# Sample attention's value products: one visit of eight quads per batch instead of four of two, and the mixed rows loaded and split at other pairs

## The chip, the cores and the metric

The kernel runs on one NeuronCore of a Trainium2 chip. A core has five engines that run side by side, each in its own program order: TensorE (PE in the profile, its weight loads PEld), VectorE (DVE), ScalarE (ACT), GpSimd (POOL) and SyncE (SP), which here issues nearly all DMAs. The metric is the device time of one execution in microseconds, the median of several runs.

## The reference, cut to what matters

One step of a decoder layer for two groups: a prompt of 1024 tokens and 8 sample batches of 4 tokens. The change is in the attention of the samples. Each sample attends to its 4096 past tokens (32 pages of 128) and its new ones; keys and values come from a cached latent of 256 numbers and a rope key of 32 per token:

```python
def one(args):                       # one sample batch
    pages, q1, c1, pe1 = args
    c_all = concatenate([pool_ckv[pages].reshape(4096, 256), c1])
    pe_all = concatenate([pool_kpe[pages].reshape(4096, 32), pe1])
    k, v = mla_keys_values(c_all, pe_all, k_pos, w_uk, w_uv, g_qk_k)
    return masked_attend(q1, k, v, q_pos, k_pos)   # 8 heads, 4 queries, softmax(q k) v
```

`k` is RMS-normalised per head (hence sums of squares of `c @ w_uk`), and `v = c @ w_uv`. The kernel never builds `v`: it multiplies the probabilities with the latents themselves and applies `w_uv` to the result.

## The kernel before, in words

The stage is `phase2b`. Its unit is a **quad**, four pages of one batch; a batch has eight quads and there are 64 in all. A **pair** is two pages, so a quad has two pairs, a batch 16 and the stage 128. The function `steps` walks over the pairs `n`, and writes down the work of each engine in the order in which it will run: PE, ACT, DVE and POOL follow that order by hand (`manual_schedule`), while SP's DMAs are placed by a planner.

For each pair `pair_score` issues 24 score matmuls on PE (line 186, tile `s`, 12 of 288 columns and 12 of 256), two squares on ACT (L1452, L1455), an addition on DVE (L1454) and, one pair later, a reduction of the squares on DVE (L1458). Every second pair starts with a rope matmul (L1422). For each quad ACT casts the latents (L1403), POOL and DVE subtract the rounded part (L1407), POOL rotates the rope key (L1392 to L1394), and ACT and DVE sum its square (L1415, L1416).

A batch's softmax (`batch_softmax`, steps r = 0 to 13) is spread over its pairs 12 to 21; pairs from 16 on belong to the next batch's scores. Steps 0 to 8 are mostly DVE work on the norms and the maximum (L1469, L247 to L261, L1476, L1479), with a scaling on POOL. Then PE transposes the maximum (r = 9, L1508, pair 19), DVE reduces it and writes it as a diagonal `dg` (r = 10, L1511 and L1513), PE spreads that over all partitions (r = 11, L1516, behind pair 20's scores), ACT copies it, POOL subtracts it (L1528) and ACT takes the exponential (L1524, pair 21).

The value products follow `LAG` = 4 pairs behind: with `v = n - 16 - LAG`, `quad_pv` multiplies a quad's probabilities with its cached rows `ck`, four matmuls of a 32-column arrangement, one per page (L1537; the profile has two records of each). The first quad of a batch has one more for the new tokens (L1535). All of a batch adds up in one PSUM bank, tile `o`. A **visit** is a stretch of such matmuls between score matmuls: now after every fourth pair, two quads each, so four visits a batch, behind its pairs 23, 27, 31 and 35 (counted from the batch's first), which are pairs 7, 11, 15 and 3 of the batch whose scores run then. After the last one `batch_out` copies `o` (ACT, L1545), sums the denominators (PE, L1549, DVE L1551 and L1555), and `batch_close` folds the result (PE L1561, ACT L1562).

The cached rows live in 15 buffers of the tag `ck`; a quad's buffer comes free when its visit is done. A column of ones in it (POOL's memset, L1284) is set shortly before the visit. The same tag also serves for other data: `mixed_load` brings in rows of another part of the layer (L1225, 384 KB, four times, one each in the score pairs of batches 1 to 4), which `split` then turns into a rounded part (ACT, L205) and a rest (DVE, L208), two halves per load. `quad_load` issues a quad's 8 page DMAs on SP (L1375 for `cT`, L1379 for `ck`), three quads ahead.

Behind pair 127 the planner also orders PE, ACT, DVE and POOL, and the work of `mem_kv` (L1605 and on) is mixed with the last batch's softmax.

Of the kernel before, what the change touches and what calls it, by code (L numbers as in the profile page):

```python
# [15 lines left out]
NB, ND = 8, 4  # L16
# [138 lines left out]
class Net:  # L155
# [1024 lines left out]
    def phase2b(self):  # L1180
        nc, tc, I = self.nc, self.tc, self.I
# [4 lines left out]
        ppt, pp = self.open("ps3t", space=PSUM), self.open("ps3", space=PSUM)  # L1186
# [10 lines left out]
        cosT, sinT, quads = self.cosT, self.sinT, self.quads  # L1197

        LAG, AHEAD = 4, 3
        last = NB * 16  # L1200
        st, ev, late = {}, {}, []

        def at(n, pos, f, *a):
            ev.setdefault((n, pos), []).append(lambda: f(*a))

        def run(n, pos):
            for f in ev.pop((n, pos), []):
                f()
# [13 lines left out]
        def mixed_load(k):  # L1222

            raw = place()[:, :768].rearrange("p (k n) -> p k n", k=2)
            nc.sync.dma_start(raw, self.mix_dram[:, k : k + 2, :384])  # L1225
            for e in range(2):
                at(8 * k + 24 + 2 * e, 3, lambda e: self.split(*(x[:, k + e] for x in self.mx0), raw[:, e], self.col("g_ab", k + e)), e)

        for k in range(0, 8, 2):
            at(8 * k + 20, 0, mixed_load, k)  # L1230
        at(last - 4, 3, lambda: self.split(*wk0, raws[0].rearrange("p (k n) -> p k n", k=8)))
        for b in range(NB):
            n = b * 16
            at(n - 10, 0, lambda b: st.__setitem__(b, self.batch_open(p, b)), b)
            at(n - 8, 2, lambda b: self.batch_enter(st[b], b), b)
            for r, (k, pos) in enumerate(((12, 0), (13, 0), (14, 0), (14, 3) if b == NB - 1 else (15, 0), (15, 0) if b == NB - 1 else (15, 3), (16, 0), (17, 0), (17, 3), (18, 2), (19, 2), (20, 0), (20, 2), (21, 3))):
                f = lambda b=b, r=r: self.batch_softmax(p, ppt, st[b], r, b == NB - 1)
                if n + k <= last:
                    at(n + k, pos, f)
                else:  # L1240
                    late.append(f)
            if b < NB - 1:
                at(n + 21, 0, lambda b=b: self.batch_softmax(p, ppt, st[b], 13, False))
            n += 16 + LAG + 15
            tail = (
                lambda b=b: self.batch_out(pt, st[b], 0),
                lambda b=b: self.batch_out(pt, st[b], 1, ppt, b == NB - 1),
                lambda b=b: self.batch_close(pt, ppt, b, st.pop(b)),
            )
            for k, pos, f in ((0, 3, tail[0]), (2, 2, tail[1]), (3 if b == NB - 2 else 4, 3, tail[2])):  # L1250
                if b < NB - 1:
                    at(n + k, pos, f)
# [4 lines left out]
        def steps(n0, n1):  # L1257
            for n in range(n0, n1):
                Q, v = n // 2, n - 16 - LAG
                if n >= 16 and n % 2 == 0 and Q + AHEAD < NB * 8:  # L1260
                    quads[Q + AHEAD] = self.quad_load(p, Q + AHEAD)
                for k, dst, src in ((2, b4, self.b_dram), (16, self.fold4, I["c_fold4"]), (64, wuv, I["w_uv"])):
                    if n == k:
                        self.behind(nc.sync.dma_start(dst, src), self.page_dma[-1])
                if n > last - 8 and n % 2 == 0 and len(raws) < 4:
                    raw = place()[:, : 8 * P]
                    src = (I["w_mk"][0], I["memT"][:, :4], I["memT"][:, 4:], I["w_mk"][1])[len(raws)]
                    nc.sync.dma_start(raw.rearrange("p (k n) -> p k n", n=src.shape[2]), src)
                    raws.append(raw)
                for pos in (-2, -1, 0):  # L1270
                    run(n, pos)
                if n % 2 == 0 and 0 <= Q + 1 < NB * 8:
                    at(n + 1, -2, self.quad_prep(quads[Q + 1]))
                    at((6, 8, 10, 10, 11)[Q + 1] if Q < 4 else n + 3, 0, self.quad_sums, Q + 1, quads[Q + 1], st[(Q + 1) // 8])
                if n % 2 and 0 <= Q + 2 < NB * 8:
                    self.quad_rot(Q + 2, quads[Q + 2], cosT, sinT)
                if n in (-1, 1, 3, 5, 7, 9, 11, 13):
                    k = Q + 4
                    rvs[k] = rvs.get(k) or self.quad_pages(k)
                    quads[k] = self.quad_load(None, k, None, rvs[k])  # L1280
                for k in {1: (0,), 3: (1,), 4: (2,), 5: (3,), 6: (4,), 7: (5,), 9: (6,), 11: (7,), 12: (8,), 13: (9,), 14: (10,)}.get(n, ()):
                    self.quad_load(p, k, quads[k], rvs.get(k))
                if n % 2 and 0 <= v + 1 < last:
                    nc.gpsimd.memset(quads[(v + 1) // 2]["ck"][:, :, 256:257], 1.0)  # L1284
                run(n, 1)
                if 0 <= n < last:
                    rope = (Q + 1, quads[Q + 1], st[(Q + 1) // 8]) if n % 2 and Q + 1 < NB * 8 else None
                    for f in self.pair_score(p, pp, n, quads[n // 2], st[n // 16], rope):
                        at(n + 1, -1, f)
                elif n == -1:  # L1290
                    self.quad_rope(self.t(pp, [P, 2, 512], F32, "s", 2)[:, 0, 320:448], 0, quads[0], st[0])()
                run(n, 2)
                if 0 <= v < last and v % 4 == 3:
                    for z in (v // 2 - 1, v // 2):
                        self.quad_pv(ppt, z, quads.pop(z), st[v // 16])
                run(n, 3)

        with tc.manual_schedule(engines={E.PE, E.Activation, E.DVE, E.Pool}):
            steps(-10, last + 1)

        with tc.manual_schedule(engines={E.SP}):
            self.close("ps3")
            for x in ("p3a", "p3c", "sq", "sm"):
                self.close(x)
            self.wr = self.open("wr", bufs=3, side="right")
            self.wp = self.open("w", bufs=3, side="right")
            mem = self.mem_kv(raws, wk0)
            for f in late[:3]:
                f()
            next(mem)  # L1310
            steps(last + 1, last + 4)
            for _ in range(5):
                next(mem)
            steps(last + 4, last + 7)
            for f in late[3:]:
                f()
            for _ in range(6):
                next(mem)
            steps(last + 7, last + 16 + LAG)
            for _ in mem:  # L1320
                pass
# [1191 lines left out]
```

## Time and profile before

| | |
|---|---|
| median of 3 runs | 1827.79 us (1826.15 to 1829.96) |
| profiled execution, span | 1823.1 us |
| sample attention, scores of batches 0 to 7 | 402 to 848 us of the span |
| matmuls of the visits (L1537) | 512 records, 380 ns each (median) |
| one mixed load to landing | 4.7 us (median of 4) |

The span is from the first to the last instruction of one execution; the median has what lies around it as well. In rows of time order the first number is the start in microseconds from the span's start, the second the duration; `xN` merges N instructions of one line; in brackets stands the engine's idle time ahead of it and what ended it. The starts of successive matmuls, and not their durations, tell what PE's time goes to, since they overlap: a score matmul lasts 0.28 to 0.30 us in the profile, but the next starts 0.12 to 0.13 later.

### The profile page before, as it was taken

The numbers are of one execution on the slowest core, as the hardware profiler recorded it, in microseconds if no ns is written. First come the engines' busy times: TensorE is split into PE (matmuls) and PEld (weight loads), VectorE is DVE, ScalarE is ACT, GpSimd is POOL, SyncE is SP. The second block draws the span as 40 slices with busy tenths as digits, with TensorE's granted clock in tenths as the row PEclk, the third lists the DMA queues.
The fourth block names the chain that finished last, engine by engine and source line by source line (L and its number), as shares of the span: only waits on it lengthen the run. The fifth ranks groups of instructions, "written<-read, shape, count | busy, mean of one in ns | idle before, by whom it ended". The sixth has DMA issues, their size and how long they took to land.

```text
span 1823.1 us, 39307 instructions
## 1 busy us (share of the span) xinstructions
PE 1800.6 (99%) x14226; PEld 1700.3 (93%) x14226; DVE 1349.6 (74%) x2796; ACT 921.5 (51%) x1910; POOL 703.0 (39%) x861
## 2 busy tenths in 40 slices
PE   9999999999999999999999999999999999999999
PEld 8999777779999999998899979999999999999999
DVE  7864767657778776777645767998888888888664
ACT  7435676766655555556433556533333333344442
POOL 1021655534545444544023010377667776400000
PEclk9999999999999999999999999999999999999999
DMA  8102354558866766664645156222222222595242
GB/s 323 47 18 70 117 176 127 165 181 227 220 201 189 202 189 181 178 180 127 194 152 188 36 197 196 71 71 94 83 71 71 83 71 85 152 325 162 85 149 78
DMA packets 153187, 261.18 MB, mean 143 GB/s; under 512 B 20897, under 2 KB 97538, under 8 KB 152994
## 3 DMA queue, kind: packets, MB, share of 16 engines
q1 hardware_dynamic: 152130, 257.63, 45.4%
q8 instruction: 112, 1.84, 0.4%
q10 hardware_dynamic: 864, 1.05, 0.2%
q14 instruction: 81, 0.66, 0.1%
HBM read 212.79 MB, written 45.82 MB: 142 GB/s over the span
## 4 chain that ended last, share of the span: by engine, by line
PE 81%; DVE 3%; ACT 1%; issue 1%; SPq 1%; POOL 1%; DMA 0%; DVEq 0%; ACTq 0%; POOLq 0%
PE s L186 22%; PE d L186 12%; PE b L186 8%; PE F L186 7%; PE X L186 7%; PE E L186 7%; PE A L186 3%; PE y L186 3%; PE o L1047 2%; PE o L1537 2%; PE tp L1032 1%; PE tp L186 1%; PE s L1422 1%; PE tp L985 1%; PE t L186 1%
## 5 line engine op out<-in xcount | busy, mean ns | idle before, releaser
L186 PE MATMUL s<-w2h,ch 128*128 128x256 f32 x1018 | 301.9, 297 | 0.5 <-ACT S L1425 0.5
L186 PE MATMUL s<-w2h,cl 128*128 128x256 f32 x1018 | 293.2, 288 | 0.0
L186 PE MATMUL s<-w2l,ch 128*128 128x256 f32 x1018 | 292.9, 288 | 0.0
L186 PEld LDWEIGHTS s<-w2h,ch 128*128 128x128 f32 x1018 | 191.5, 188 | 8.9 <-issue 3.7
L186 PEld LDWEIGHTS s<-w2l,ch 128*128 128x128 f32 x1018 | 191.7, 188 | 0.0
L186 PEld LDWEIGHTS s<-w2h,cl 128*128 128x128 f32 x1018 | 191.3, 188 | 0.0
L1458 DVE TENSOR_REDUCE ss<-sq 128x16 f32<-128x1024 f32 x128 | 155.3, 1213 | 29.8 <-ACT sq L1455 29.4
L1407 POOL TENSOR_TENSOR cl<-cT,ch 128x512 fp32r<-128x512 f32 x64 | 83.5, 1304 | 185.6 <-ACT ch L1403 185.4
L1455 ACT ACTIVATE sq<-s 128x512 f32<-128x512 f32 x128 | 76.6, 598 | 82.7 <-PE s L186 82.7
L1452 ACT ACTIVATE sq<-s 128x512 f32<-128x512 f32 x128 | 76.9, 601 | 75.9 <-PE s L186 70.9
L201 ACT CAST a<-brb 128x528 fp32r<-128x528 f32 x77 | 48.8, 634 | 110.5 <-PE d L186 104.6
L186 PE MATMUL d<-a,w 128*128 128x264 f32 x768 | 95.2, 284 | 0.0
L202 DVE TENSOR_TENSOR a<-brb,a 128x528 fp32r<-128x528 f32 x77 | 54.1, 704 | 55.2 <-ACT a L201 55.1
L186 PEld LDWEIGHTS d<-a,w 128*128 128x128 f32 x768 | 94.3, 188 | 0.0
L2149 POOL TENSOR_TENSOR lo<-s,hi 128x1024 fp32r<-128x1024 f32 x20 | 64.0, 3200 | 45.7 <-ACT hi L2148 45.7
L186 PE MATMUL mm<-whi,xh 128*128 128x256 f32 (+3 forms) x272 | 77.1, 285 | 0.0
L2204 ACT COPY a<-A 128x264 f32<-128x264 f32 x43 | 16.1, 375 | 120.6 <-PE A L186 114.2
L186 PE MATMUL mm<-wlo,xh 128*128 128x256 f32 (+3 forms) x272 | 76.8, 285 | 0.1
L186 PE MATMUL mm<-whi,xl 128*128 128x256 f32 (+3 forms) x272 | 76.8, 286 | 0.0
L1403 ACT CAST ch<-cT 128x512 fp32r<-128x512 f32 x128 | 73.5, 629 | 0.0
L2270 POOL TENSOR_TENSOR cv<-cv,row 128x1056 f32<-128x1056 f32 x22 | 65.1, 2960 | 21.0 <-ACT cv L2269 21.0
L186 PE MATMUL d<-a,hi 128*128 128x264 f32 x552 | 72.0, 284 | 0.0
(755 smaller groups left out, 6348.1 us busy)
## 6 DMA issues: line engine op xcount, KB each, us to landing
cT<-cT SPq DMA_DIRECT2D x256, 160.0 KB, 2.8
ck<-ck SPq DMA_DIRECT2D x256, 144.0 KB, 3.4
raw<-w_up SPq DMA_DIRECT2D x44, 512.0 KB, 3.5
wsumd<-wsum SPq DMA_DIRECT2D x26, 512.0 KB, 3.9
actd<-cv SPq DMA_DIRECT2D x44, 264.0 KB, 2.4
brb<-actd SPq DMA_DIRECT2D x44, 264.0 KB, 5.7
wsum<-w_down SPq DMA_DIRECT2D x22, 512.0 KB, 3.8
raw<-wsumd SPq DMA_DIRECT2D x20, 512.0 KB, 3.7
```

The source lines that it names most:

```text
L186: x = self.nc.tensor.matmul(out, l, r, start=first and i == 0, stop=last and i == len(seq) - 1)
L201: first = {"act": nc.scalar.copy, "pool": nc.gpsimd.tensor_copy, "dve": nc.vector.tensor_copy}[eng](hi, src)
L202: low = lambda: nc.vector.tensor_tensor(lo, src, hi, ALU.subtract)
L1047: nc.tensor.matmul(u["o"][g : g + 64, o : o + m * P], s["v"][:, j, h % 4], th[:, z * P : (z + m) * P], start=j == 0, stop=b == len(banks) - 1,
L1403: nc.scalar.copy(d["h"][:, k], src[k])
L1407: (nc.vector if k else nc.gpsimd).tensor_tensor(d["l"][:, k], src[k], d["h"][:, k], ALU.subtract)
L1452: nc.scalar.activation(sq[:, 0], ps[:, :, n0 : n0 + 256], AF.Square)
L1455: nc.scalar.activation(sq[:, 1], pt.rearrange("p (e d) -> p e d", e=2), AF.Square)
L1458: yield lambda: nc.vector.tensor_reduce(s["ss"][:, g0 : g0 + 2].rearrange("p e (z h) -> p z e h", z=2), sq.rearrange("p z e (h d) -> p z e ...
L1537: nc.tensor.matmul(s["o"][j * 32 : j * 32 + 32], S[:, q * 4 + j], d["ck"][:, j, :257], start=q == 0 and j > 0, stop=q == 7)
L2149: eng.tensor_tensor(lo, src, hi, ALU.subtract)
L2270: nc.gpsimd.tensor_tensor(cv, cv, row, ALU.mult)
```

## The change

All eight quads of a batch are multiplied in one visit, where the first of the four visits stood (`v % 16 == 3`, pair 23 from the batch's first, which is pair 7 of the next one). Batch 6 (`NB - 2`) does six quads there and holds two for `v % 16 == 15`. `batch_out` and `batch_close` come 12 pairs earlier, except for batch 6. The memset of the ones comes 12 pairs earlier per quad. The mixed rows are loaded at pair `8k + 24` instead of `8k + 20`, and their halves are split at pairs `8k + 26` and `8k + 27` instead of `8k + 24` and `8k + 26`.

```diff
             for e in range(2):
-                at(8 * k + 24 + 2 * e, 3, lambda e: self.split(*(x[:, k + e] for x in self.mx0), raw[:, e], self.col("g_ab", k + e)), e)
+                at(8 * k + 26 + e, 3, lambda e: self.split(*(x[:, k + e] for x in self.mx0), raw[:, e], self.col("g_ab", k + e)), e)
 
         for k in range(0, 8, 2):
-            at(8 * k + 20, 0, mixed_load, k)
+            at(8 * k + 24, 0, mixed_load, k)
...
-            n += 16 + LAG + 15
+            n += 16 + LAG + (15 if b == NB - 2 else 3)
...
-                if n % 2 and 0 <= v + 1 < last:
-                    nc.gpsimd.memset(quads[(v + 1) // 2]["ck"][:, :, 256:257], 1.0)
+                if n % 2 and 0 <= n - 7 < last:
+                    nc.gpsimd.memset(quads[(n - 7) // 2]["ck"][:, :, 256:257], 1.0)
...
-                if 0 <= v < last and v % 4 == 3:
-                    for z in (v // 2 - 1, v // 2):
-                        self.quad_pv(ppt, z, quads.pop(z), st[v // 16])
+                if 0 <= v < last and v % 16 in (3, 15):
+                    b, held = v // 16, 2 if v // 16 == NB - 2 else 0
+                    for z in range(b * 8, b * 8 + 8 - held) if v % 16 == 3 else range(b * 8 + 8 - held, b * 8 + 8):
+                        self.quad_pv(ppt, z, quads.pop(z), st[b])
```

## The prediction, made before the change was run

> **What bounds the kernel now.** I read the page's head first, then the busy time by stretches, the order of time on PE, and the order of time on DVE.
>
> ```profile
> span 1823.1 us, 39307 instructions
> PE 1800.6 (99%) x14226; PEld 1700.3 (93%) x14226; DVE 1349.6 (74%) x2796; ACT 921.5 (51%) x1910; POOL 703.0 (39%) x861
> ...
> 536.00:592.00 56.00, 56.00 (x473) 52.66 (x472) 42.29 (x81) 33.26 (x73) 26.64 (x43) 1.00 0.65 187
> ```
>
> The last row is one batch of sample attention, 16 pairs and four visits (columns: PE, PEld, DVE, ACT, POOL busy, granted clock, DMA). PE is busy for all 56 us at full clock, DVE for 42. So here a microsecond taken from PE's order of work shortens the kernel, as long as DVE, ACT and the loads keep up with a PE that comes sooner. Those two questions are the whole sum. The times below are of this execution (span 1823.1); the median of the runs is 1827.79, 4.69 more, and I carry that difference.
>
> **What a visit costs.** PE in order of time around one two-quad visit (start, duration), a row of the chain of waits (the 24 score matmuls of a pair), and a four-quad and an eight-quad visit later on:
>
> ```profile
> 550.62 0.28 PE L186 MATMUL s<-w2h,cl 128*128 128x256 f32 x1
> 550.83 1.07 PE L1537 MATMUL o<-ck,S 128*32 128x257 f32 x16
> 551.84 0.40 PE L186 MATMUL s<-w2h,ch 128*128 128x288 f32 x1
> 552.07 0.29 PE L186 MATMUL s<-w2l,ch 128*128 128x288 f32 x1
> ...
> 830.40 3.00 PE s L186 x24
> ...
> 847.49 1.94 PE L1537 MATMUL o<-ck,S 128*32 128x257 f32 x32
> ...
> 878.78 0.40 PE L1535 MATMUL o<-cn,S 128*32 128x257 f32 x1
> ...
> 879.03 3.84 PE L1537 MATMUL o<-ck,S 128*32 128x257 f32 x61
> ```
>
> From 550.62 to 552.07 are 1.45 us; without the visit two ordinary steps of 3.00/24 = 0.125 would stand there, so it costs 1.20. The four-quad visit is 1.94 against 1.07: two quads more cost 0.87, one quad 0.435. Hence 0.87 of the 1.20 is work that stays wherever it is done, and **0.33 is paid once per visit**: it begins 0.21 after the last score matmul instead of 0.125, and behind it the second score starts 0.23 after the first. The eight-quad visit of the last batch runs 878.78 to 882.87, 4.09 us. By these prices it is 8 x 0.435 plus 0.20 (1.07 less 0.87) plus its new-token matmuls (L1535), 0.41 by what is left, so the price per quad holds in a long visit.
>
> **Removed.** In batches 0 to 5 three of four visits go: 18 x 0.33 = 5.94 us. In batch 6 six quads go at pair 7 and two stay for later:
>
> ```profile
> 833.40 1.00 PE o L1537 x16
> ...
> 850.23 0.36 PE L1605 MATMUL b<-mh,wk0h 128*128 128x256 f32 x1 [0.80 <-DVE S L1454]
> ...
> 851.13 0.47 DVE L208 SCALAR_TENSOR_TENSOR ml<-ck,cols,mh 128x256 fp32r<-128x256 f32 x1
> ```
>
> The first row is of the chain of waits. The visit at 833.4 goes (0.33 saved). The one at 847.5 loses two of its four quads, but PE then stands 0.80 us for DVE, which starts L208 only at 851.13, so these 0.87 us were covered. Moved to pair 7 they lie open. Batch 6 therefore costs +0.54; if ACT's copy of o, which stands behind that visit, sets the end there, it saves 0.33 instead. I take +0.54, since DVE is the later one. Batch 7 had one eight-quad visit already. PE gains 5.94 - 0.54 = 5.4.
>
> **Moved on PE.** batch_close's four L1561 stood right behind a visit, and L1508 right before one:
>
> ```profile
> 537.65 0.63 PE L1561 MATMUL m<-fold,oo 128*128 128x32 f32 x4
> 538.12 0.38 PE L186 MATMUL s<-w2h,ch 128*128 128x288 f32 x1
> 538.33 0.29 PE L186 MATMUL s<-w2l,ch 128*128 128x288 f32 x1
> ...
> 466.10 0.27 PE L1508 MATMUL m<-ident,mx 128*32 128x128 f32 x1
> ...
> 466.34 0.30 PE L186 MATMUL s<-w2l,ch 128*128 128x288 f32 x1
> ```
>
> L1561 is followed by a first score step of 0.21 instead of 0.125, as a visit is by one of 0.23. Together they paid that once, apart they pay twice: 6 x 0.10 = 0.6 back. L1508 alone is seen in batch 0: the row at 466.34 is the second score behind it, 0.24 after its start, where 0.125 would do, so alone it costs 0.11 and no switch like a visit's. **PE's own saving: 5.94 - 0.54 - 0.6 = 4.8 us.**
>
> L1508's row also says 128*32, the visit's own arrangement. [...]
>
> **Given back: DVE before L1516.** PE waits in L1516 (pair 20, counted from the batch's start) for dg, the end of DVE's softmax chain. A visit at pair 11, 15 or 19 gives DVE time to catch up. First PE and DVE of batch 0, which has no visit in these pairs, then batch 1 with two behind pair 12 (ACT's L1455 is a pair's last square, DVE's L1458 its reduction):
>
> ```profile
> 469.27 0.86 DVE L1513 TENSOR_SCALAR dg<-ident,mm 32x32 f32<-32x32 f32 x1
> 470.19 0.40 PE L1516 MATMUL m<-dg,ones 32*128 32x32 f32 x2 [0.81 <-DVE dg L1513]
> ...
> 494.33 0.60 ACT L1455 ACTIVATE sq<-s 128x512 f32<-128x512 f32 x1 [0.83 <-PE s L186]
> 495.11 1.20 DVE L1458 TENSOR_REDUCE ss<-sq 128x16 f32<-128x1024 f32 x1
> 496.34 1.26 DVE L1469 TENSOR_TENSOR ss<-ss,kss 128x192 f32<-128x192 f32 x1
> 498.53 0.60 ACT L1455 ACTIVATE sq<-s 128x512 f32<-128x512 f32 x1 [0.76 <-PE s L186]
> 499.42 1.21 DVE L1458 TENSOR_REDUCE ss<-sq 128x16 f32<-128x1024 f32 x1
> 512.84 1.22 DVE L1458 TENSOR_REDUCE ss<-sq 128x16 f32<-128x1024 f32 x1 [0.24 <-ACT sq L1455]
> 517.78 0.22 DVE L1454 TENSOR_TENSOR S<-s,S 128x64 f32<-128x64 f32 x1 [0.44 <-ACT sq L1452]
> 522.36 1.22 DVE L1458 TENSOR_REDUCE ss<-sq 128x16 f32<-128x1024 f32 x1 [0.68 <-ACT sq L1455]
> 523.80 0.23 DVE L1513 TENSOR_SCALAR dg<-ident,mm 32x32 f32<-32x32 f32 x1
> 525.95 0.40 PE L1516 MATMUL m<-dg,ones 32*128 32x32 f32 x2
> ```
>
> Call lag the time from L1455 to L1458 of a pair. Batch 1, pair 12: 499.42 - 498.53 = 0.89. From there DVE needs until 524.03, 24.61 us, of which 0.24 + 0.44 + 0.68 are idle: 23.25 of work. PE reaches L1516 at 498.53 + 27.42; without two visits of 1.20 that is 25.02. So PE will wait lag + 23.25 - 25.02, that is **lag at pair 12 less 1.77 us**. From pair 11 to 12 DVE works 499.42 - 495.11 = 4.31, and PE without a visit takes 498.53 - 494.33 - 1.20 = 3.00, so the lag grows by 1.31. At pair 11:
>
> ```profile
> 526.06 0.60 ACT L1455 ACTIVATE sq<-s 128x512 f32<-128x512 f32 x1 [0.76 <-PE s L186]
> 526.69 1.22 DVE L1458 TENSOR_REDUCE ss<-sq 128x16 f32<-128x1024 f32 x1 [0.46 <-ACT sq L1455]
> ...
> 547.70 0.60 ACT L1455 ACTIVATE sq<-s 128x512 f32<-128x512 f32 x1 [0.24 <-PE s L186]
> 549.53 0.68 DVE L1407 TENSOR_TENSOR cl<-cT,ch 128x512 fp32r<-128x512 f32 x1
> 550.13 1.21 DVE L1458 TENSOR_REDUCE ss<-sq 128x16 f32<-128x1024 f32 x1
> ...
> 442.58 0.49 DVE L1469 TENSOR_TENSOR ss<-ss,kss 128x192 f32<-128x192 f32 x1
> ```
>
> A DVE that has caught up has 0.63 (526.69 - 526.06). That is batches 5 and 6: 0.63 + 1.31 = 1.94, a wait of 0.17 each. In batches 1 to 4 the second mixed split now stands at pair 11, right ahead of the softmax (before: pairs 8 and 10). The split at pair 10 shows what it does: DVE waits for ACT's half, runs L208, and the lag is 2.43, less L1407's 0.60, which pair 11 does not have: 1.83. Then the wait is 1.83 + 1.31 - 1.77 = 1.37. That has L1469 at the 1.26 of batch 1; in batch 0 it took 0.49, which makes it 0.60. I take 0.60, because a later DVE meets it at another moment than the slow one; 0 and 1.37 remain the ends. **Back: 4 x 0.60 + 2 x 0.17 = 2.7 us.**
>
> **Cost at nothing.** The memsets (L1284) keep their number and their place in POOL's order and only serve a quad six loads younger; POOL is busy 26.64 of 56 us. The mixed splits keep number and size. ACT's copy of o now waits through a 4.1 us visit, with pair 24's casts (L1403) behind it; PE has two pairs, 6 us, to run before it needs those. Without that cover the wait itself, up to 4.1 us in each of six batches, would be PE's. The loads:
>
> ```profile
> ck<-mix SPq DMA_DIRECT2D x4, 384.0 KB, 4.7
> ...
> 531.77 1.91 SPq L1375 DMA_DIRECT2D cT<-cT  x4
> 537.32 2.85 SPq L1379 DMA_DIRECT2D ck<-ck  x4
> ```
>
> Today the mixed load goes ahead of quad 14's, whose ck load then stands until the visit at 536 frees a buffer (531.77 + 1.91 to 537.32). After, this load need not wait, and the mixed one is issued behind quad 15's, just after the visit. It has three pairs, some 9 us; the list of DMA issues has it landing 4.7 us after its issue, so I cost it at nothing. If it came later than ACT's turn by more than a pair, PE would stand too.
>
> **Sum:** -4.8 + 2.7 = -2.1: span 1821.0, time 1825.7.
>
> **Rivals.**
> - *Full saving* (0.30). DVE's work between the same points shrinks when L1469 and its kind aren't held up (0.49 against 1.26), and PE finds dg ready: -4.8 gives 1823.0 (-5.7 with batch 6's better end, 1822.1). Against it: batch 0's wait of 0.81, with no visit in between.
> - *DVE becomes the bound* (0.14), the other side. The place is L1513. In batch 0 it took 0.86 instead of 0.23. If it does so in all six batches, 6 x 0.63 = 3.8 more; with the mixed batches at 1.37, 5.8 + 3.8 - 4.8 = +4.8: 1832.5; with them at 0.60, +1.7. It decides from a mean wait of 0.8 us at L1516, just what batch 0 shows; for it speaks that ACT's copy of o no longer stands in front of the casts at pair 19, against it batch 0's higher load.
> - *Lone L1508 pays a switch* (0.04): 6 x 0.33 = 2.0 back, 1827.7. Batch 0's row speaks against it. [...]
> - *The visits don't join* (0.03): the 0.33 is paid per quad. Then nothing is won and 2.7 lost, 1830.5; the x32 and x61 rows speak against it.
>
> **Chances.** The forecast, part given back (-0.5 to -4.0), has 0.49. Two tenths of a per cent, 3.7 us, is about what a measurement of this kernel can tell from no change. Faster by over that: the full saving's 0.30 and 0.09 of the forecast's best end, 0.39. Slower by over that: 0.08 of the DVE rival and 0.02 of the fourth, 0.10. Within: 0.51. The range reaches from the full saving with a little over (1822.3) to the lighter form of the DVE rival (1829.6); the forecast's own is 1823.8 to 1827.3.
>
> **What would show it.** Right: nine contiguous visits, the eight-quad ones near 4.1 us, steps of 0.21 and 0.23 around them as now; pairs between visits unchanged; waits before L1516 of 0.6 in batches 1 to 4 and next to none in 5 and 6; the lag at pair 12 near 1.9 and 2.4 to 3.1. Wrong: no waits at L1516 (full saving), waits over 0.8 (DVE), or PE idle at pairs 26 to 29 behind L205, which would be a late mixed load, or idle at 848 to 885 that grows, since that part is put in order by a planner and may come out otherwise.

## The result, and the profile after

The changed kernel is a little slower. Its median is 1831.01 us (1826.38 to 1834.37, 22 runs), that of the kernel before, beside it, 1827.59 us (1824.72 to 1830.17, 22 runs). The ratio is 1.0019, with a 95% interval of 1.0013 to 1.0025: 3.4 us more (2.4 to 4.6), where 2.1 us less was forecast. That lies outside the forecast's range. Some 0.45 us of it lies outside the span: an execution of after lasts 2.2 us longer than its span, one of before 1.7. Why isn't shown.

The profiled execution of after, the page's span and its line of engines:

```profile
span 1828.7 us, 39333 instructions
...
PE 1799.9 (98%) x14226; PEld 1704.5 (93%) x14226; DVE 1346.0 (74%) x2796; ACT 918.2 (50%) x1910; POOL 702.3 (38%) x861
```

Three rows of its list of waits:

```profile
engine line waited for: us in total, times, longest us
...
ACT S L1426 <- DVE S L1455: 38.0, 31, 2.3
...
ACT oo L1546 <- PE o L1538: 21.2, 7, 3.4
...
PE m L1517 <- DVE dg L1514: 6.4, 7, 1.0
```

The list of waits of before has, for the first two:

```profile
ACT S L1425 <- DVE S L1454: 12.2, 17, 2.5
...
ACT oo L1545 <- PE o L1537: 4.2, 7, 0.9
```

From line 1296 on, after's line numbers are one higher than before's: L1517 is L1516, L1514 is L1513, L1408 is L1407. PE's matmul L1517 now waits for dg in seven batches, 6.4 us in all. Before, it waited in batch 0 alone. ACT's rope copy L1426 waits 38 us for VectorE, where it waited 12.2.

What these waits look like, in the timeline of after (start, length, engine, line; pair 20 of batch 3, then the visit behind pair 23; here and below, rows of other work in between are left out):

```profile
641.53 0.21 DVE L1455 TENSOR_TENSOR S<-s,S 128x64 f32<-128x64 f32 x1
641.66 1.21 DVE L1459 TENSOR_REDUCE ss<-sq 128x16 f32<-128x1024 f32 x1
641.78 0.27 ACT L1426 COPY S<-s 128x128 f32<-128x128 f32 x1 [1.22 <-DVE S L1455]
641.94 1.14 ACT L1404 CAST ch<-cT 128x512 fp32r<-128x512 f32 x2
642.64 1.27 POOL L1408 TENSOR_TENSOR cl<-cT,ch 128x512 fp32r<-128x512 f32 x1 [2.86 <-ACT ch L1404]
642.79 0.27 DVE L1512 TENSOR_REDUCE mm<-m 32x1 f32<-32x128 f32 x1
643.10 0.85 DVE L1514 TENSOR_SCALAR dg<-ident,mm 32x32 f32<-32x32 f32 x1
644.00 0.40 PE L1517 MATMUL m<-dg,ones 32*128 32x32 f32 x2 [0.94 <-DVE dg L1514]
...
654.05 0.40 PE L1536 MATMUL o<-cn,S 128*32 128x257 f32 x1
...
654.30 3.84 PE L1538 MATMUL o<-ck,S 128*32 128x257 f32 x61
```

The visit is as forecast: 654.05 to 658.14, 4.09 us. But L1514 takes 0.85 us, not 0.23, and ends at 643.95, when POOL's L1408 has just ended (642.64 + 1.27 = 643.91). It is so in all seven batches, and the rows show why it comes back each time. One VectorE instruction, L1455, starts two chains. By ACT (L1426, L1404) it leads to POOL's L1408. By VectorE (L1459, L1512) it leads to L1514, 0.45 to 0.46 us behind L1408's start in each of them. Before, ACT did not wait for L1455 at this place: it stood in its copy of o (L1545) first. The timeline of before, batch 1:

```profile
522.88 0.38 ACT L1545 COPY oo<-o 128x257 f32<-128x257 f32 x1 [0.55 <-PE o L1537]
523.14 0.27 ACT L1425 COPY S<-s 128x128 f32<-128x128 f32 x1
524.01 1.30 POOL L1407 TENSOR_TENSOR cl<-cT,ch 128x512 fp32r<-128x512 f32 x1 [4.29 <-ACT ch L1403]
```

Here dg started first and took 0.23; POOL started 0.02 us before it ended (523.80 + 0.23).

Batch 1 lost more. Its mixed rows came late. After (SPq is SyncE's DMA queue):

```profile
488.49 1.93 SPq L1376 DMA_DIRECT2D cT<-cT  x4
491.20 3.34 SPq L1380 DMA_DIRECT2D ck<-ck  x4
494.64 0.39 SPq L1225 DMA_DIRECT2D ck<-mix  x1
...
498.32 0.62 ACT L205 ACTIVATE mx0h<-ck,cols 128x384 fp32r<-128x384 f32 x1 [1.16 <-DMA ck<-mix]
```

The load was issued at 494.64, eight microseconds behind the visit's end (486.9), because SyncE's queue had the eight page loads above to hand out first.

**Where the time went.** The starts of ACT's last square of a pair (L1455, after L1456) measure it, from pair 23, the end of batch 0, to pair 119. The timeline of before:

```profile
480.27 0.60 ACT L1455 ACTIVATE sq<-s 128x512 f32<-128x512 f32 x1 [0.82 <-PE s L186]
...
818.92 0.60 ACT L1455 ACTIVATE sq<-s 128x512 f32<-128x512 f32 x1 [0.82 <-PE s L186]
```

The same two squares in the timeline of after:

```profile
482.89 0.60 ACT L1456 ACTIVATE sq<-s 128x512 f32<-128x512 f32 x1 [0.82 <-PE s L186]
...
823.75 0.60 ACT L1456 ACTIVATE sq<-s 128x512 f32<-128x512 f32 x1 [0.82 <-PE s L186]
```

That is 338.65 and 340.86: 2.2 us more in batches 1 to 6. Three visits fewer in each should give -5.9 (6 x 0.99). The waits at L1517 in these batches (0.98, 1.02, 0.94, 1.03, 0.77, 0.80) add 5.5, batch 1 another 1.6, batches 2 to 4 together 0.9, batches 5 and 6 together 0.1. From pair 119 to the end of the last visit after is 0.75 longer.

The same measure for every kernel of the study, as differences to the first profile of before (us). Batch 1 runs from pair 23 to 39, the others likewise:

| kernel | batch 1 | batches 2-4 | batches 5, 6 | ratio to before (95%) |
|---|---|---|---|---|
| after | +1.6 | +0.9 | -0.3 | 1.0019 (1.0013-1.0025) |
| after_again | +4.1 | +1.1 | -0.3 | a single run |
| visits_alone | +0.3 | -0.6 | -0.4 | 1.0002 (0.9993-1.0011) |
| visits_alone_again | +0.4 | -0.5 | -0.1 | 1.0003 (0.9993-1.0012) |
| mixed_alone | +0.4 | 0.0 | 0.0 | 1.0013 (1.0004-1.0022) |
| mixed_alone_again | +2.0 | 0.0 | 0.0 | 1.0008 (0.9999-1.0017) |
| load_early_split_late | +0.7 | +1.0 | -0.1 | 1.0010 (1.0001-1.0019) |
| six_and_two | +2.6 | -0.1 | -1.1 | 1.0008 (1.0000-1.0017) |
| cl_behind_dg | +2.4 | -0.8 | -1.5 | 1.0000 (0.9991-1.0009) |
| dg_earlier | +1.2 | -2.5 | -2.0 | 0.9978 (0.9969-0.9987) |
| dg_earlier_old_mixed | -0.6 | -3.0 | -2.0 | 0.9977 (0.9968-0.9986) |
| repairs_again | -0.5 | -3.0 | -2.0 | 0.9977 (0.9968-0.9986) |
| all_eight_in_batch_6 | -0.6 | -3.0 | -2.0 | 0.9971 (0.9960-0.9982) |
| before_dg_earlier | 0.0 | 0.0 | 0.0 | 0.9994 (0.9984-1.0004) |

The four profiles of before agree within 0.01 us in batches 1 to 6, so before's own scatter is no part of these columns. Two profiles of one changed kernel differ by up to 0.3 us in batches 2 to 6 and by up to 2.5 in batch 1. In batch 0 the profiles of before differ by up to 1.0 us, and the first one was the shortest.

### The profile page after: what moved, and what is told of

The parts are those of the page before. It is cut to its first block, busy times and chain, and to the rows that moved or that the text cites. A ratio compares the mean times of both kernels' runs of the same rounds, so it can differ in the third digit from the quotient of the medians.

```text
span 1828.7 us, 39333 instructions
## 1 busy us (share of the span) xinstructions
PE 1799.9 (98%) x14226; PEld 1704.5 (93%) x14226; DVE 1346.0 (74%) x2796; ACT 918.2 (50%) x1910; POOL 702.3 (38%) x861
## 4 chain that ended last, share of the span: by engine, by line
PE 72%; DVE 10%; issue 2%; ACT 2%; SPq 2%; DMA 1%; POOL 1%; DVEq 0%; ACTq 0%; POOLq 0%
PE s L186 13%; PE d L186 12%; PE b L186 8%; PE F L186 7%; PE X L186 7%; PE E L186 7%; PE A L186 3%; PE y L186 3%; DVE ss L1459 3%; PE o L1047 2%; PE o L1538 2%; PE tp L1032 1%; PE tp L186 1%; DVE cl L1408 1%; SPq L1376 1%
## 5 line engine op out<-in xcount | busy, mean ns | idle before, releaser
L1459 DVE TENSOR_REDUCE ss<-sq 128x16 f32<-128x1024 f32 x128 | 155.1, 1212 | 29.3 <-ACT sq L1456 29.3
L1408 POOL TENSOR_TENSOR cl<-cT,ch 128x512 fp32r<-128x512 f32 x64 | 83.2, 1300 | 209.5 <-ACT ch L1404 209.4
L1456 ACT ACTIVATE sq<-s 128x512 f32<-128x512 f32 x128 | 76.4, 597 | 67.1 <-PE s L186 67.1
L1455 DVE TENSOR_TENSOR S<-s,S 128x64 f32<-128x64 f32 x128 | 27.8, 217 | 67.8 <-ACT sq L1453 67.8
L1404 ACT CAST ch<-cT 128x512 fp32r<-128x512 f32 x128 | 73.5, 627 | 0.2 <-issue 0.2
```

Of the source, the lines that this page charges most:

```text
L1404: nc.scalar.copy(d["h"][:, k], src[k])
L1408: (nc.vector if k else nc.gpsimd).tensor_tensor(d["l"][:, k], src[k], d["h"][:, k], ALU.subtract)
L1456: nc.scalar.activation(sq[:, 1], pt.rearrange("p (e d) -> p e d", e=2), AF.Square)
L1459: yield lambda: nc.vector.tensor_reduce(s["ss"][:, g0 : g0 + 2].rearrange("p e (z h) -> p z e h", z=2), sq.rearrange("p z e (h d) -> p z e ...
```

## The experiments

**1. The change taken apart.** Theory W: the waits at L1517. Rival M: the mixed rows. Rival T: the tail. First the visits without the move of the mixed rows:

```
-                at(8 * k + 26 + e, 3, lambda e: self.split(
+                at(8 * k + 24 + 2 * e, 3, lambda e: self.split(
...
-            at(8 * k + 24, 0, mixed_load, k)
+            at(8 * k + 20, 0, mixed_load, k)
```

> The eight-quad visits with the mixed rows at their old pairs (loaded at pair 4, split at pairs 8 and 10 of a batch). Time before 1827.6, after 1831.0. Theory W (PE's waits at L1517, 0.8 to 1.0 us in each of seven batches, eat the visits' saving; the mixed rows only add batch 1's late load): the waits at L1517 stay near 0.9 each, the 1.2 us that batch 1 loses between its pairs 9 and 15 goes, 1829 to 1830.5. Rival M (the later mixed rows are the whole cost): the waits at L1517 fall under 0.3, 1823 to 1825. Rival T (only the tail behind pair 119 lost): 1830.5 to 1831.5 with the waits as after.

Its list of waits:

```profile
PE m L1517 <- DVE dg L1514: 5.4, 7, 0.9
```

1827.47 us beside 1826.94, ratio 1.0002. The waits stay, 0.62 to 0.94 each, so the visits by themselves win next to nothing, as W says; M's value is missed, and T's too, since the time is 3 us under that of after. But the time lies under W's 1829 as well: the move of the mixed rows cost more than its 1.2 us in batch 1. Then the reverse, the kernel before with the mixed rows moved:

> The kernel before with the mixed rows loaded four pairs later and split in pairs 10 and 11, visits as before. Theory W: with a visit at pairs 11, 15 and 19 VectorE still catches up, the waits at L1516 in batches 1 to 6 stay under 0.3, 1827.5 to 1828.5. Rival M: 1830 to 1831.5, with waits at L1516 or at pairs 26 to 29.

1829.33 us, ratio 1.0013: more than W gave it and less than M. It has no waits at L1516 outside batch 0. Batch 1 alone is longer, by 0.4 us in this profile and 2.0 in the second one (below). Neither theory had put so much on this part.

**2. The dg step earlier in VectorE's order.** L1512 and L1514 go three positions forward in the schedule. By the timelines that brings them ahead of one VectorE instruction, the L1459 of 1.2 us that stood in front of them; L1417, which the expectation counts in, was not between them.

```
-... (18, 2), (19, 2), (20, 0), (20, 2), (21, 3))):
+... (18, 2), (19, 2), (19, 3), (20, 2), (21, 3))):
```

> After, with the step that makes dg (L1512, L1514) three positions earlier in VectorE's order: behind TensorE's transpose in pair 19, ahead of pair 19's L1459 and L1417. It takes 1.3 us of VectorE's queue out from in front of dg and moves L1514 away from POOL's L1408. Theory W: the waits at L1517 go (7 x 0.92 = 6.4 us), 1824.5 to 1826. Rival U (VectorE as a whole is the bound, so the order inside its queue does not matter): the waits move to the pairs behind, 1830 to 1831.5.

The timeline of this kernel, same place as above:

```profile
635.92 0.27 DVE L1512 TENSOR_REDUCE mm<-m 32x1 f32<-32x128 f32 x1
636.22 0.23 DVE L1514 TENSOR_SCALAR dg<-ident,mm 32x32 f32<-32x32 f32 x1
...
636.89 1.28 POOL L1408 TENSOR_TENSOR cl<-cT,ch 128x512 fp32r<-128x512 f32 x1 [2.86 <-ACT ch L1404]
637.20 0.40 PE L1517 MATMUL m<-dg,ones 32*128 32x32 f32 x2
```

dg is ready 0.75 us before PE wants it, and no batch waits. 1823.33 us, ratio 0.9978: faster than after by over 7 us and than before by 4. VectorE has the same work and only its order differs, so rival U falls. In batches 5 and 6 the gain is 1.0 us each: three visits at 0.33.

**3. A visit given back ahead of L1517.** The edit below goes with one more: `batch_out` and `batch_close` come 12 pairs later again, as in before.

```
-                    b, held = v // 16, 2 if v // 16 == NB - 2 else 0
+                    b, held = v // 16, 2 if v // 16 < NB - 1 else 0
```

> After, with every batch but the last in two visits, as batch 6 has them: six quads behind pair 23, two behind pair 35, which is pair 19 of the next batch, right ahead of L1517. Theory W: VectorE gets its 1.2 us back where it needs them and the waits at L1517 in batches 1 to 6 go under 0.2; two visits instead of four save 2 x 0.33 in six batches, 4 us, against before, 1824 to 1825.5. Rival U: 1829 to 1831, the waits stay.

The waits went in batches 1 to 6, as W says, though L1514 still took 0.86 to 0.87 us: the visit of 1.2 us covered it. The timeline, batch 3:

```profile
637.12 0.38 ACT L1546 COPY oo<-o 128x257 f32<-128x257 f32 x1 [0.55 <-PE o L1538]
637.83 0.27 ACT L1426 COPY S<-s 128x128 f32<-128x128 f32 x1 [0.33 <-DVE S L1455]
638.69 1.29 POOL L1408 TENSOR_TENSOR cl<-cT,ch 128x512 fp32r<-128x512 f32 x1 [2.86 <-ACT ch L1404]
639.14 0.87 DVE L1514 TENSOR_SCALAR dg<-ident,mm 32x32 f32<-32x32 f32 x1
```

ACT's copy of o stands in front of the rope copy again, as in before, and L1426 waits for L1455 all the same. So the meeting of L1514 with L1408 doesn't come from the missing copy, but from a VectorE that is late. The time was missed: 1828.33 us, ratio 1.0008. Batches 5 and 6 gained 0.57 and 0.55, near 2 x 0.33, batches 2 to 4 nothing, and batch 1 lost 2.6, with this line in its list of waits:

```profile
PE s L186 <- DVE cl L1408: 1.5, 1, 1.5
```

ACT stood 2.86 us for the late mixed rows there, VectorE behind ACT, and PE behind VectorE. So the mixed rows cost something outside L1517 too.

**4. Only the meeting of L1514 and POOL's L1408.** VectorE's order as in after; POOL's half of L1408 in pair 21 is made to wait for dg:

```
+                x = (nc.vector if k else nc.gpsimd).tensor_tensor(...)
+                dg, self.dg = getattr(self, "dg", None), None
+                if dg:
+                    self.tc.add_manual_dep(x.ins, dg.ins.name, ...)
```

> After, with one wait added: POOL's half of L1408 in pair 21 starts only when dg (L1514) is done. VectorE's order is as after. Theory P (L1514 takes 0.85 instead of 0.23 because POOL's L1408 runs beside it): L1514 takes 0.23 in all seven batches, the waits at L1517 fall from 0.92 to 0.3 each, 7 x 0.62 = 4.3 us, 1826.5 to 1828. Rival Q (L1514 is slow for another reason, such as its place behind L1512): it stays at 0.85 and the kernel at 1830.5 to 1832, the added wait included.

The timeline of this kernel (its L1519 is dg, L1522 is PE's matmul):

```profile
638.97 0.23 DVE L1519 TENSOR_SCALAR dg<-ident,mm 32x32 f32<-32x32 f32 x1
639.25 0.40 PE L1522 MATMUL m<-dg,ones 32*128 32x32 f32 x2 [0.36 <-DVE dg L1519]
639.37 1.28 POOL L1408 TENSOR_TENSOR cl<-cT,ch 128x512 fp32r<-128x512 f32 x1 [3.72 <-DVE dg L1519]
639.69 1.51 DVE L1408 TENSOR_TENSOR cl<-cT,ch 128x512 fp32r<-128x512 f32 x1
```

The dg instruction takes 0.23 in all seven batches and the waits are 0.20, 0.36, 0.40, 0.36, 0.41, 0.18, 0.14. 1826.60 us, ratio 1.0000, 3.5 us less than after's ratio. Theory P holds, with 0.62 us for each batch. The long VectorE instruction is now its half of L1408, 1.51 us where after's took 0.67 at this place, but nothing of PE waits for that.

**5. Load or split?** After, with the load at its old pair and the splits at the new ones:

> After, with the mixed rows loaded at their old pair (4 of a batch) and split at the new ones (10 and 11). visits_alone, with both at the old pairs, gave 1827.5 beside a before of 1826.9; after lost 3.4 to before. Theory L (the late load is what costs): the extra of batch 1 goes and batches 2 to 4 lose nothing, ratio to before 1.0000 to 1.0008. Theory S (the two splits in neighbouring pairs 10 and 11, right ahead of the softmax, keep VectorE 2 us behind at pair 12): only batch 1's 1.3 us goes, ratio 1.0008 to 1.0015, lag at pair 12 still near 2.1 in batches 2 to 4.

How far VectorE is behind at pair 12 of batch 2, from L1456 to L1459. The timeline of this kernel:

```profile
559.53 0.60 ACT L1456 ACTIVATE sq<-s 128x512 f32<-128x512 f32 x1 [0.56 <-PE s L186]
...
561.66 1.21 DVE L1459 TENSOR_REDUCE ss<-sq 128x16 f32<-128x1024 f32 x1
```

And of visits_alone:

```profile
560.04 0.60 ACT L1456 ACTIVATE sq<-s 128x512 f32<-128x512 f32 x1 [0.76 <-PE s L186]
...
561.65 1.21 DVE L1459 TENSOR_REDUCE ss<-sq 128x16 f32<-128x1024 f32 x1
```

2.13 against 1.61. Theory S: the splits in pairs 10 and 11 keep VectorE half a microsecond later, and batches 2 to 4 lose as much as in after. Batch 1 loses 0.7, where after lost 1.6 and 4.1: the rest was the load. The ratio, 1.0010, lies in S's range, but its interval (1.0001 to 1.0019) holds most of L's too; what decides is the columns of the batches.

**6. Both repairs**, dg earlier and the mixed rows at their old pairs, and the earlier dg in the kernel before:

> Both repairs together: dg three positions earlier (ratio 0.9978 alone) and the mixed rows at their old pairs (after against visits_alone: 1.0019 against 1.0002). If the two are separate, 0.9978 - 0.0017 = 0.9961, some 1820 beside a before of 1827. If the mixed rows only cost through the wait at L1517, which is then gone, it stays at 0.9978, except for batch 1's late load, 1.2 us: 0.9971.

> The kernel before with dg three positions earlier alone. Theory W: only batch 0 waits at L1516 there, so 0.81 us and no more, ratio 0.9993 to 1.0000. Rival: the earlier dg helps any kernel by itself and the visits have no part in it: 0.9975 to 0.9985.

> Both repairs once more, beside the one before: 0.9977 with 0.9968 to 0.9986 the first time. Expected 0.9970 to 0.9982, and no wait at L1517 in any batch.

Both repairs give 1822.34 and 1822.11 us, ratio 0.9977 each time (0.9968 to 0.9986), and PE waits at L1517 in no batch of either profile. In batches 2 to 6 every batch is 0.97 to 1.02 us shorter than before's, 3 x 0.33. ACT still waits for VectorE almost as in after, and it costs nothing:

```profile
ACT S L1426 <- DVE S L1455: 31.1, 34, 2.5
```

The profile shows 1.7 us less in batch 1 than with dg earlier alone and 0.5 less in batches 2 to 4, but the timed ratios, 0.9977 and 0.9978, don't tell the two apart; that stays open. What the interval rules out is 0.9961, the value for two separate costs. In the kernel before the earlier dg gives 0.9994, its interval holding 1: only batch 0 had a wait to lose. So the gain is the visits', and the earlier dg lets it through.

**7. Batch 6 in one visit too**, on top of both repairs:

> Both repairs (dg earlier, mixed rows at their old pairs), and batch 6 too in one visit of eight quads. One visit less is 0.33 us. Theory: 0 to 0.5 us beside the two repairs alone, no difference to be measured; the tail behind pair 119 keeps its order. Rival T (two quads held back fill a gap of TensorE's in the tail, and the planner orders the tail otherwise without them): 1 to 3 us slower.

1821.70 us, 0.9971 (0.9960 to 0.9982): not told from the two repairs. Two quads held back are worth nothing that can be measured.

**8. A stretch at half the clock.** Most profiles have a stretch of 3.4 us at half the granted clock between 840 and 880 us. These runs ask whether it is part of the loss:

> The kernel after, a second profile. Open is whether the stretch of 3.4 us at half the granted clock, which every profile with the new visits shows once between 840 and 880 us (0.83 in a window of 10 us, so 1.7 us), belongs to them. If it does: again one, with the waits at L1517 again 0.77 to 1.03. If it falls by chance: none, or at another place, and the waits the same. The late mixed load of batch 1 may come out otherwise by a microsecond.

> The kernel before, a second profile. If the stretch at half the clock between 840 and 880 us belongs to the changed kernels: none again. If it falls by chance: it may show one, 1.7 us, and then that much of the difference between the two profiles is nothing of the change.

> The kernel before, a third profile. So far its two profiles show no stretch at half the granted clock between 840 and 880 us, and the two of after show one each (1.6 to 1.7 us). If the stretch belongs to the changed kernels: none here. If it falls by chance: each profile of before has some chance of it, and one of this and the next should show it.

> The kernel before, a fourth profile, expected as the third: no stretch at half the granted clock between 840 and 880 us if it belongs to the changed kernels, one in this or the third if it falls by chance.

> The mixed rows moved alone, a second time: ratio 1.0013 (1.0004 to 1.0022) the first time, of which the profile put 1.0 us in the stage up to pair 119 and 1.5 us in the stretch at half the clock behind it. If that stretch belongs to the kernel: again one, ratio 1.0008 to 1.0018. If it falls by chance: it may be missing, and the ratio falls to 1.0002 to 1.0010. Batch 1's late load is there in either case.

> The joined visits with the mixed rows at their old pairs, a second time: ratio 1.0002 (0.9993 to 1.0011) the first time, though its profile was 2.9 us longer than before's from pair 0 on, 2.3 of it behind pair 119. If the stretch at half the clock belongs to the kernel: again one, and the ratio rises to 1.0005 to 1.0012. If it falls by chance: it may be missing, and the ratio stays at 0.9996 to 1.0005.

The third profile of before has it, in windows of 1 us (the third column from the right is the granted clock):

```profile
874.00:875.00 1.00, 1.00 (x7) 0.86 (x8) 1.00 (x2) 0.00 (x0) 0.00 (x0) 1.00 0.42 157
...
876.00:877.00 1.00, 1.00 (x4) 0.81 (x3) 0.82 (x6) 0.73 (x1) 0.00 (x0) 0.50 0.80 292
877.00:878.00 1.00, 1.00 (x4) 0.81 (x3) 0.44 (x3) 0.00 (x0) 0.00 (x0) 0.50 0.00 0
```

So it can come without the change. All eleven profiles of kernels with joined visits have it, and two of the seven with the visits as before: it isn't bound to the change, but came more often with it. Why was not tried. In after it falls here:

```profile
855.00:856.00 1.00, 0.00 (x0) 0.00 (x0) 1.00 (x4) 1.00 (x3) 0.00 (x0) 1.00 0.86 111
...
857.00:858.00 1.00, 1.00 (x6) 1.00 (x6) 1.00 (x4) 1.00 (x3) 0.47 (x1) 0.50 1.04 426
```

PE has stood idle, and VectorE and ACT are busy without a break (fourth and fifth numbers, 1.00). In both profiles of after it lies there, and the stretch to the end of the last visit is only 0.75 longer than in before; where it lies at 873 to 880, as in visits_alone, it is 2.3 longer. The timed executions have no trace, but each has its mean granted clock. Among the 107 of before that were timed beside the experiments, an execution with a mean clock lower by 0.001 is 1.2 us longer; the mean over the 22 of after is lower than theirs by 0.0004. So, as an estimate, such stretches make up some 0.5 us of after's 3.4. visits_alone came out at 1.0003 (0.9993 to 1.0012) the second time, with the stretch: it came again, but the ratio did not rise as it should have if the stretch were the kernel's cost. mixed_alone came out at 1.0008 without it, as expected if it falls by chance.

A second profile of after repeats the waits at L1517 (0.98, 1.02, 0.98, 1.02, 0.80, 0.80 in batches 1 to 6). Its batch 1 was worse:

```profile
499.59 0.61 ACT L205 ACTIVATE mx0h<-ck,cols 128x384 fp32r<-128x384 f32 x1 [3.69 <-DMA ck<-mix]
...
501.51 0.40 PE L186 MATMUL s<-w2h,cl 128*128 128x288 f32 x1 [1.93 <-DVE cl L1408]
```

ACT stood 3.69 us and PE then 1.93; the batch lost 4.1 us.

## Why the prediction was wrong

**The price of a visit: right.** 0.33 us per visit was shown by the kernels without waits at L1517: 0.97 to 1.02 for three. The long visit's 4.09 us was the forecast 4.1. That a lone L1508 pays no switch holds as well; a switch of 0.33 in each batch would have left 0.66 of these.

**"Apart they pay twice": wrong.** With 0.10 back in each batch, only 0.89 would have been left of 0.99. The kernel with both repairs has L1562 (L1561 in before) alone between scores:

```profile
551.73 0.53 PE L1562 MATMUL m<-fold,oo 128*128 128x32 f32 x4
...
552.31 0.29 PE L186 MATMUL s<-w2l,ch 128*128 128x288 f32 x1
```

From its start to the second score behind it are 0.58 us; behind a visit, in the prediction's rows, they were 0.68 (537.65 to 538.33). What the lone one pays behind it, it saves in front: in after its second matmul starts 0.03 us behind its first (727.68 and 727.71), in before, behind a visit, 0.13 (537.65 and 537.78). The 0.6 of the sum was not there.

**The wait at L1516: here the forecast failed, in one term.** With the collision taken out (experiment 4) the waits in batches 5 and 6 were 0.18 and 0.14, forecast 0.17, and in batches 1 to 4 0.36 to 0.41, forecast 0.60. That they came so near is in part luck. The lag at pair 12 was 1.6 in batches 5 and 6, not 1.94, and by "lag less 1.77" PE would not have waited there; VectorE needed 23.5 to 23.6 us from pair 12's L1459 to the end of dg, not 23.25. The one error took off 0.3, the other put it back. In batches 2 to 4 the lag was 2.1, under the 2.4 to 3.1 that was to show the forecast right.

What failed was to leave L1514 at 0.23. It was known from batch 0 that it could take 0.86, and this was put into a rival with a chance of 0.14, as something that batch 0's load brought about. It was no matter of batch 0: L1514 took 0.84 to 0.85 in all seven batches of after. Where VectorE was late, one instruction of it set off both POOL's L1408 and, 0.45 to 0.46 us later, L1514. That is 6 x 0.62 = 3.7 us on top of the 1.9 of experiment 4, and the waits are 5.5 instead of 2.7. The rival had the place and the price (0.63); its reason, that ACT's copy of o is gone from in front of the casts, is not enough (experiment 3). Its point of decision, 0.8 us at L1516, was passed with 0.92 on the mean, and its two values, +1.7 and +4.8, lie on either side of the 3.4 measured.

**Cost at nothing, the mixed load: wrong in batch 1.** "Issued just after the visit" was so in batches 2 to 4, where both profiles have it within 1.1 us of the visit's end. In batch 1 it was issued eight microseconds later, and ten in the second profile, behind page loads that were still to be handed out, and ACT waited 1.16 and 3.69 us in two profiles. It was named as what would make the prediction wrong, but with no price and no chance. Of the parts of the sum this is the one that varies.

**Cost at nothing, the splits: wrong by a little.** In batches 2 to 4 the splits at pairs 10 and 11 cost 0.2 to 0.4 us a batch besides the wait at L1517; no single row shows it, load_early_split_late against visits_alone does.

**Right at nothing:** the memsets, and ACT's wait of up to 3.4 us for the long visit, 21.2 us in all, behind which no wait of PE appears.

**Batch 6 and the tail.** +0.54 was forecast, and from pair 119 to the end of the last visit after is 0.75 longer. The planner cut the two held quads into three pieces there, where one visit was forecast, so that PE made eleven visits in all, not nine. The reason given, that moved work would no longer cover PE's wait for VectorE, is in the row: 1.52 us, where before's had 0.80.

```profile
856.14 0.36 PE L1606 MATMUL b<-mh,wk0h 128*128 128x256 f32 x1 [1.52 <-DVE S L1455]
```

The sum as it should have been, for batches 1 to 6 and the tail: -5.9 + 5.5 + 1.0 + 0.75, and batch 1's load, 1.6 to 4.1: +3.0 to +5.5. Measured were 3.4, the 0.45 outside the span included, so the timed executions lie at the lower end of this sum.

## What to carry to other kernels

Before a piece of work is taken out in front of a wait, ask what the other engines did with that time; here the visit of 1.2 us was the slack in which VectorE caught up, and the gain came only when dg's place in VectorE's order was moved as well (0.9978 instead of 1.0019). The small instruction that ends a chain belonged, in this kernel, where its input was ready, not behind work that nobody waits for. And a load that is put "just behind" something has to be looked up in the queue of the busiest batch, not in a typical one.

## What was not expected of the hardware

L1514, a VectorE instruction of 0.23 us in batches 1 to 7 of before, took 0.84 to 0.85 in the seven batches of after in which it started 0.45 to 0.46 us behind POOL's L1408, and ended 0.03 behind it in each. In experiment 4, where POOL's L1408 waited for it, it took 0.23. VectorE's half of L1408 took 1.51 us beside POOL's in experiment 4, and 0.67 behind it in after. The 128 reductions (L1459) stayed at 1.19 to 1.24 in after, among them the 32 that ran beside POOL's L1408 for over 0.3 us. What made the two instructions longer, and left the reductions alone, isn't shown.

The stretch at half the granted clock (0.50) lasts 3.4 us, sits in different places in two profiles of one kernel (from 876.7 us in visits_alone, from 873.9 in visits_alone_again), and comes in some executions and not in others (before has none between 840 and 880 us, before_third has one). In after, stretches at 0.50 start at 235.31 and at 856.54 us; the 621.23 between the starts are 182 times the length, 3.413. In after PE had stood idle for 1.52 us shortly ahead of the stretch, until 856.14; in before_third PE is busy just ahead of it (1.00 of the microsecond from 874). What brings the stretch isn't shown.
